# The MLP's first stage by seven products on two levels, with its outer sums kept in SBUF

## Chip, cores and metric

One core of one Trainium2 chip runs the kernel. The metric is the device time of one execution in microseconds (us). The engines are called as in the profile: PE (TensorE, matmuls; PEld its weight loads), ACT (ScalarE), DVE (VectorE), POOL (GpSimd) and SP (SyncE, which only issues DMAs here). Each engine has one queue of instructions.

## The reference

A decoder block on x of 2048 tokens x 1024 channels, all in float32. Attention and a gated MLP branch are merged, projected and added to x (this makes x1); then comes the part that the change is about:

```
h = _rmsnorm(x, norm_pre_mlp[layer])
a = jax.nn.relu(jnp.einsum('bsd,df->bsf', h, w_mlp_in[layer]))
y = jnp.einsum('bsf,fd->bsd', a * a, w_mlp_out[layer])
x = x + _rmsnorm(y, norm_post_mlp[layer])
```

D_FF is 4096. So the MLP's first stage multiplies 2048 x 1024 by 1024 x 4096, takes relu and square, and the second stage multiplies the result by 4096 x 1024.

## The kernel before

Every float32 product is made of three matmuls: each operand is split into a rounded high part (a copy, on ACT as a rule) and the rest (a subtraction, on DVE or POOL); high x high, high x low and low x high are added up in PSUM. The helper `split` (L70 copy on ACT, L72 on POOL, L78 subtraction on DVE or POOL) does it everywhere, so its lines stand for many tiles. `split_in` (L91) loads and splits.

*Part 2* (merge and output). For four chunks of 512 tokens, in the order 2, 3, 0, 1, `merge` makes the gated sum of the branches in eight steps `dt` of 18 matmuls, and `out_block` makes four blocks of 128 tokens of 48 matmuls each: it loads the rows of x (tile xr, SP, L1233), adds the normed product (DVE L1257), stores x1 (POOL's queue, L1260), norms again, and later (`flush`) transposes the result and stores it as h2 in DRAM. `sums_t` loads quarters of h2, makes four sums on POOL (L1291 to L1294) and stores them (POOL's queue, L1296) for the Strassen operands of the MLP. Outside PE the order of this part is the scheduler's; `behind()` puts what is written under it behind the latest instruction of each queue.

*MLP, first stage.* Seven products in place of eight (Strassen in Winograd's form): the contraction is halved (k 0..3 and 4..7 of 128 channels), tokens are halved within each 1024 (512 each), and features go in pairs of 128 (q, 16 pairs). For each half of the tokens and each q, `product` (L1428) makes seven products of 4 x 3 = 12 matmuls of 128x512. The stationary operands are sums of weight blocks (`add_a`: POOL, L1399 to L1402; splits in `split_a`), the moving ones (B11, B21, T1..T4, B22) sums of h2. Products are added up partly in PSUM and partly by DVE (L1453, L1457); each of the four results gets Relu and Square on ACT (L1437, L1438) and is stored to DRAM as s by a DMA that ACT issues (L1434).

*MLP, second stage.* Seven products again, over s and w_mlp_out: `yproduct` (L1957) makes one product of 2 x 3 = 6 matmuls, then DVE adds it to an accumulator (L1962) before PE may write the same bank again. A step is seven products, 42 matmuls, in the order 1, 2, 6, 7, 5, 4, 3; three steps overlap. `sum_s` prepares the stationary sums of the step three ahead: copy and subtraction of 128x768, four POOL sums of 128x256 (L1757 to L1760), two copies and subtractions of 128x512. `ops_of` splits the moving operands of the next group, `sum_w2` (L1713 to L1717) makes their sums on POOL. From here on all queues follow the order in which the code is written (`as_written`):

```
    def as_written():
        t = mybir.EngineType
        return tc.manual_schedule(engines={t.Activation, t.DVE, t.Pool, t.SP})
```

Of the kernel before, what the change touches and what calls it, by code (L numbers as in the profile page):

```python
# [16 lines left out]
P = 128  # L17
S = 2048
D = 1024
# [22 lines left out]
def block_kernel(ctx, tc, a, out):  # L42
# [104 lines left out]
    t_d = dtile([2, P, 4, 4, 512], "td")  # L147
# [985 lines left out]
    gtp = stack(e2, "gtp", 2)  # L1133
# [148 lines left out]
    def sums_t(half, k, pl, tag, tag2, bufs2):  # L1282

        w = pl.tile([P, 2, 512], F32, name=f"tq{half}{k}", tag=tag, bufs=1)
        b11, b12 = w[:, 0], w[:, 1]
        b21, b22 = ((wp3 if pl is not ttp else pl).tile([P, 512], F32, name=f"tq{half}{k}{n}", tag=tag2, bufs=bufs2)
                    for n in range(2))
        t0 = half * HALF
        for t, kk, c in ((b11, k, 0), (b12, k, 1), (b22, k + 4, 1), (b21, k + 4, 0)):
            sp.dma_start(t, h2_d[:, kk, t0 + c * 512:t0 + c * 512 + 512])  # L1290
        pool.tensor_sub(b11, b12, b11)  # L1291
        pool.tensor_sub(b12, b22, b12)
        pool.tensor_sub(b22, b22, b11)
        pool.tensor_sub(b21, b21, b22)  # L1294
        for name, t in (("T1", b11), ("T3", b12), ("T2", b22), ("T4", b21)):
            pool.dma_start(t_d[half][:, T_AT.index(name), k], t)  # L1296

    def merge_sums(dt):
        if dt == 3:
            sums_ahead(0)  # L1300

    def merge_sums_last(dt):
        if dt == 3:
            sums_ahead(3)

    def sums_ahead(k):
        with behind():
            sums_t(1, k, ttp, "tq", "tr", 2)

    chunks = (2, 3, 0, 1)  # L1310
    FIRST = ((0, 0), (1, 0), (0, 1), (2, 0), (1, 1))
    e3, er = ExitStack(), ExitStack()
    cnt = [0]

    def psum_any(name):
# [5 lines left out]
    TERMS = {1: ("A11", "B11"), 2: ("A12", "B21"), 3: ("S4", "B22"), 4: ("A22", "T4"),  # L1321
             5: ("S1", "T1"), 6: ("S2", "T2"), 7: ("S3", "T3")}
    NQ, LEAD, TRAIL = NF // 2, 5, 3
    b_, a_, araw, bank, xs_, u_, c1_, n_u, alone_, sums_ = {}, {}, {}, {}, {}, {}, {}, [0], {}, {}

    def load_b(half, name):

        w = r3.tile([P, 2, 4, 512], F32R, name=f"{name}_{half}", tag=name, bufs=1)
        for k in range(0, 4, 2):
            t0, k0 = half * HALF, k + (4 if name == "B21" else 0)  # L1330
            split_in(w[:, :, k:k + 2], h2_d[:, k0:k0 + 2, t0:t0 + 512], None, "act")
# [774 lines left out]
```

## Time and profile before

| | |
|---|---|
| time, median of 3 runs | 2644.91 us (2641.12 to 2645.22) |
| the profiled execution: span | 2646.3 us |
| PE busy | 2614.2 us (99%), 12458 matmuls |
| DVE, POOL, ACT busy | 1659.3, 1195.3, 1092.9 us |
| part 2 | some 1064 to 1398 us from the start |
| MLP, first stage (L1428) | 1398.6 to 2014 us |
| MLP, second stage (L1957, L1939) | 2014 to 2636 us |

A row of groups reads: line, engine, operation, tiles out<-in, partitions x elements, count | busy us in total, mean ns of one | idle time before them and what ended it. A row of a time-ordered list reads: start, duration (us), engine, line, operation, tiles, count, and in brackets the idle time before it with its releaser; several instructions in a row with one name are merged, and their duration is the whole stretch. ACTq, SPq are the sequencers, which issue DMAs. Matmuls overlap, so a single one looks longer (389 ns) than the distance between two.

### The profile page before, as it was taken

The numbers are of one execution on the slowest core, as the hardware profiler recorded it, in microseconds if no ns is written. First come the engines' busy times: TensorE is split into PE (matmuls) and PEld (weight loads), VectorE is DVE, ScalarE is ACT, GpSimd is POOL, SyncE is SP. The second block draws the span as 40 slices with busy tenths as digits, with TensorE's granted clock in tenths as the row PEclk, the third lists the DMA queues.
The fourth block names the chain that finished last, engine by engine and source line by source line (L and its number), as shares of the span: only waits on it lengthen the run. The fifth ranks groups of instructions, "written<-read, shape, count | busy, mean of one in ns | idle before, by whom it ended". The sixth has DMA issues, their size and how long they took to land. (4 is left out here: it accounts for less than half of the span.)

```text
span 2646.3 us, 35496 instructions
## 1 busy us (share of the span) xinstructions
PE 2614.2 (99%) x12458; PEld 2184.1 (83%) x12458; DVE 1659.3 (63%) x2797; ACT 1092.9 (41%) x2286; POOL 1195.3 (45%) x1082
## 2 busy tenths in 40 slices
PE   9999999999999999999999999999999999999998
PEld 8888888788888877888877888888888888888886
DVE  5676665534443456765667664655438888888866
ACT  5213111254455344544446555655545333323334
POOL 0363354364454554211324572233225677666645
PEclk9999999999999999999999999999999999999999
DMA  8779778988898899744556464744443221222235
GB/s 321 286 243 330 258 233 286 299 278 257 290 292 227 231 292 348 261 140 167 213 194 252 155 219 143 230 124 124 123 136 108 88 85 60 88 88 88 88 117 210
DMA packets 389572, 527.25 MB, mean 199 GB/s; under 512 B 57041, under 2 KB 242129, under 8 KB 388370
## 3 DMA queue, kind: packets, MB, share of 16 engines
q1 hardware_dynamic: 300624, 434.98, 49.8%
q0 software_dynamic: 14992, 51.65, 5.1%
q10 hardware_dynamic: 73778, 38.35, 4.8%
q8 instruction: 98, 1.61, 0.2%
q14 instruction: 80, 0.66, 0.1%
HBM read 341.72 MB, written 183.17 MB: 198 GB/s over the span
## 5 line engine op out<-in xcount | busy, mean ns | idle before, releaser
L1957 PE MATMUL ya<-T_spots,s 128*128 128x512 f32 x1176 | 289.3, 389 | 0.7 <-ACT T_spots L70 0.5
L70 ACT ACTIVATE s<-sraw 128x768 fp32r<-128x768 f32 (+1 forms) x184 | 127.2, 696 | 330.4 <-POOL sraw L1758 155.7
L1957 PEld LDWEIGHTS ya<-T_spots,s 128*128 128x128 f32 x1176 | 220.5, 188 | 47.4 <-ACT T_spots L70 0.9
L78 DVE TENSOR_TENSOR s<-sraw,s 128x512 fp32r<-128x512 f32 x172 | 184.2, 1095 | 8.5 <-ACT s L70 5.9
L1428 PE MATMUL aa<-B,A 128*128 128x512 f32 x768 | 182.3, 390 | 1.5 <-ACT xs L1442 0.9
L1399 POOL TENSOR_TENSOR s<-w1r 128x512 f32<-128x512 f32 x32 | 42.4, 1324 | 306.7 <-DVE S L78 260.1
L724 PE MATMUL g<-opA,spots 128*128 128x512 f32 x672 | 170.8, 398 | 2.3 <-DVE cv L756 1.8
L1428 PEld LDWEIGHTS aa<-B,A 128*128 128x128 f32 x768 | 143.8, 188 | 32.1 <-ACT xs L1442 1.3
L724 PE MATMUL g<-opB,spots 128*128 128x512 f32 x648 | 164.0, 397 | 0.0
L1957 PE MATMUL yc<-T_spots,s 128*128 128x512 f32 x624 | 159.6, 389 | 0.0
L95 PE MATMUL x<-hT_a,wq 128*128 128x512 f32 x384 | 149.7, 390 | 0.0
L96 PE MATMUL x<-hT_a,wq 128*128 128x512 f32 x384 | 149.4, 389 | 0.0
L97 PE MATMUL x<-hT_a,wq 128*128 128x512 f32 x384 | 149.4, 389 | 0.0
L724 PEld LDWEIGHTS g<-opA,spots 128*128 128x128 f32 x672 | 120.9, 188 | 24.7 <-issue 2.2
L78 POOL TENSOR_TENSOR spots<-gr,spots 128x512 fp32r<-128x512 f32 x98 | 128.5, 1315 | 23.1 <-DMA gr<-in_w_in_dram 8.8
L1957 PEld LDWEIGHTS yc<-T_spots,s 128*128 128x128 f32 x624 | 117.1, 188 | 24.3
L724 PEld LDWEIGHTS g<-opB,spots 128*128 128x128 f32 x648 | 116.9, 188 | 21.2
L70 ACT ACTIVATE hl<-r 128x512 fp32r<-128x512 f32 x48 | 30.4, 633 | 236.5 <-POOL r L325 89.0
L974 DVE TENSOR_REDUCE o<-po 128x256 f32<-128x512 f32 x48 | 33.2, 691 | 133.1 <-PE po L973 133.1
L72 POOL TENSOR_SCALAR spots<-gr 128x512 fp32r<-128x512 f32 x86 | 55.4, 645 | 133.5 <-PE g L724 92.2
L1757 POOL TENSOR_TENSOR sraw<-sraw 128x256 f32<-128x256 f32 x56 | 41.9, 748 | 161.8 <-DVE s L78 158.8
L78 POOL TENSOR_TENSOR T_spots<-w2r,T_spots 128x512 fp32r<-128x512 f32 x70 | 104.4, 1519 | 7.3 <-ACT T_spots L70 7.3
(430 smaller groups left out, 6965.1 us busy)
## 6 DMA issues: line engine op xcount, KB each, us to landing
w1r<-in_w_mlp_in_dram SPq DMA_DIRECT2D x64, 512.0 KB, 3.7
sraw<-sd SPq DMA_DIRECT2D x128, 256.0 KB, 3.2
qk<-hl SPq DMA_DIRECT2D x24, 1024.0 KB, 5.6
qq<-qk SPq DMA_DIRECT2D x96, 256.0 KB, 5.2
w2r<-in_w_mlp_out_dram SPq DMA_DIRECT2D x16, 1024.0 KB, 7.9
sd<-u ACTq DMA_DIRECT2D x63, 256.0 KB, 3.7
g<-gated SPq DMA_DIRECT2D x56, 256.0 KB, 5.3
gr<-sgd SPq DMA_DIRECT2D x53, 256.0 KB, 4.5
```

The lines of the kernel that those rows point to most:

```text
L70: act.activation(hi, src, AF.Copy)
L72: pool.tensor_scalar(hi, src, 1.0, 1.0, op0=OP.mult, op1=OP.mult)
L78: (pool if lo_eng == "pool" else dve).tensor_sub(lo, src, f32(hi))
L95: pe.matmul(ps, lh, rh, start=start, stop=False)
L96: pe.matmul(ps, lh, rl, start=False, stop=False)
L97: pe.matmul(ps, ll, rh, start=False, stop=stop)
L724: pe.matmul(p, w[:, l, k], h[:, r, k], start=i in (1, 6, 5, 4) and not k and not m, stop=k == 3 and m == 2, skip_group_check=True)
L974: dve.tensor_reduce(ot[:, :, j * 64:(j + 1) * 64], po.rearrange("p (b h e) -> p b e h", b=4, h=2), axis=AX.X, op=OP.add)
L1399: pool.tensor_add(s1, a21, a22)
L1428: pe.matmul(p, w[:, l, k, :], h[:, r, k, :], start=i in (1, 6, 5) and not k and not n, stop=k == 3 and n == 2, skip_group_check=True)
L1757: pool.tensor_add(a22, a21, a22)
L1957: pe.matmul(p, s[:, l], w[r], start=i in (1, 2, 5) and not m and not o, stop=m == 1 and o == 2, skip_group_check=True)
```

## The change

The first stage gets two levels. The outer level halves the contraction (k), the tokens (1024 each) and the features (16 tiles of 128 each) and makes seven outer products, in the order 1, 2, 6, 5, 3, 7, 4. Each outer product has eight inner steps (`hsteps`), one for each pair of feature tiles, and each inner step is again seven products, over two blocks of 128 channels, 512 tokens and 128 features, of 6 matmuls each (`hproduct`). So a step has 42 matmuls, and it is laid out as in the second stage: the same TIMES, three steps overlapping, `sum_ha` for the stationary sums of the step three ahead, `ops_hb` and `sum_w2` for the moving operands of the next outer product, all queues in written order.

The results of the outer products are kept in sixteen SBUF tiles X of 128x1024: outer product 1 writes X, 6 adds to it, 5 makes its own sum in a staging tile, which POOL adds to X and SP stores to DRAM (m5), and 7 adds to X. 2, 3, 7 and 4 finish outputs: in these, each of the four results of a step gets Relu, Square and a store that ACT issues. Before 4, m5 is loaded and POOL subtracts it from X again (`m5_sub`). In 1 and 5, the first product of each place is copied out of PSUM by ACT; all others are added by DVE.

The weight sums of the outer level (S1 to S4) are made in part 2 by sixteen `w_piece` (POOL) and stored to DRAM; two `t_piece` make the inner token sums for the first outer product. `next_piece` is called after the steps dt 4 and 7 of a merge and after each output block of the first three chunks. The outer token sums (tq) are made by POOL during the first outer product (`outer_load`, `outer_sums`, `outer_store`). The second stage's own products are as before; its tiles lie elsewhere.

The core of the diff (of functions that are not shown, `load_ha` loads a step's weights, `load_hb` an outer product's moving operands, `t_piece` is like `w_piece` for h2, and the old first stage is removed):

```diff
-    t_d = dtile([2, P, 4, 4, 512], "td")
+    t_d = dtile([P, 2, 4, 512], "td")
+    tq_d = {n: dtile([P, 4, 1024], f"tq{n}d") for n in ("T1", "T2", "T3", "T4")}
+    ws_d = dtile([NF // 4, P, 4, 2, 512], "wsd")
+    m5_d = dtile([NF // 4, P, 4, 512], "m5d")
     s_d = dtile([NF // 2, 2, P, 4, 4, P], "sd")
...
+    T_AT, WS_AT = ("T1", "T3", "T4", "T2"), ("S2", "S4", "S3", "S1")
...
+    def w_piece(t):
+        w, v = (ttp.tile([P, 2, 512], F32, name=f"{n}w{t}", tag=n, bufs=1) for n in ("tq", "tr"))
+        for z, n in ((v, t + NF // 2), (w, t)):
+            sp.dma_start(z.rearrange("p a c -> p (a c)"), a["w_mlp_in"][n].rearrange("p k c -> p (k c)"))
+        a11, a12, a21, a22 = w[:, 0], w[:, 1], v[:, 0], v[:, 1]
+        q, f = divmod(t, 2)
+        pool.tensor_add(a22, a21, a22)
+        pool.tensor_sub(a21, a11, a21)
+        pool.dma_start(ws_d[q][:, 2:4, f], v)
+        pool.tensor_sub(a11, a22, a11)
+        pool.tensor_sub(a12, a12, a11)
+        pool.dma_start(ws_d[q][:, 0:2, f], w)
+    W_PIECES = [(w_piece, t) for t in range(NF // 2)]
+    pieces = deque(W_PIECES[:13] + [(t_piece, 0), (t_piece, 1)] + W_PIECES[13:])
+    def next_piece():
+        if pieces:
+            f, n = pieces.popleft()
+            with behind():
+                f(n)
+    def merge_pieces(dt):
+        if dt in (4, 7):
+            next_piece()
+    def last_pieces(dt):
+        if dt in (1, 3, 5):
+            next_piece()
 
...
+    NQ, HQ = NF // 2, NF // 4
+    OPS = ("B11", "B21", "T2", "T3", "T1", "T4", "B22")
+    USE = {1: (0, "B11"), 2: (1, "B21"), 6: (2, "T2"), 7: (3, "T3"), 5: (4, "T1"), 4: (5, "T4"), 3: (6, "B22")}
+    S_AT = {1: 0, 2: 1, 4: 2, 6: 3, 5: 4, 7: 5, 3: 6}
...
+    PLACE = {1: (0, 0), 2: (0, 0), 6: (0, 1), 3: (0, 1), 4: (1, 0), 7: (1, 1), 5: (1, 1)}
+    OUTER = ((1, "A11"), (2, "A12"), (6, "S2"), (5, "S1"), (3, "S4"), (7, "S3"), (4, "A22"))
+    OUTER_B = ("B11", "B21", "T2", "T1", "B22", "T3", "T4")
+    hsteps = [(o, q) for o in range(7) for q in range(HQ)]
+    NH = len(hsteps)
...
+    def sum_ha(n):
+        w = ring(n, f"hs_{n}", [P, 2, 7, 256])
+        raw = hraw_.pop(n)
+        hs_[n] = w
+        split(w[:, 0, :3], w[:, 1, :3], raw[:, :3], "act", "dve")
+        yield
+        a11, a12, a22, a21 = (raw[:, k] for k in range(4))
+        pool.tensor_add(a22, a21, a22)
+        pool.tensor_sub(a21, a11, a21)
+        pool.tensor_sub(a11, a22, a11)
+        pool.tensor_sub(a12, a12, a11)
+        yield
+        for to, k in (((4, 6, 1), (2, 4, 1)), ((3, 7, 3), (0, 2, 1))):
+            to, k = slice(*to), slice(*k)
+            split(w[:, 0, to], w[:, 1, to], raw[:, k], "act", "dve")
+            yield
...
+    def ops_hb(o, j, engs=("dve", "pool")):
+        for m, eng in enumerate(engs):
+            op_w2(key(o, m), OPS[j], eng)
+    def sum_w2(q, part, eng=None):
+        r, e = w2r_[q], eng or pool
+        if part == 0:
+            e.tensor_sub(r[:, 4], r[:, 1], r[:, 0])
+            e.tensor_sub(r[:, 1], r[:, 3], r[:, 1])
+        if part in (1, 2):
+            e.tensor_sub(r[:, 0], r[:, 3], r[:, 4])
+        if part in (1, 3):
+            e.tensor_sub(r[:, 2], r[:, 2], r[:, 0])
...
+    outer_t = {}
+    def outer_load(n):
+        k, c = n % 4, n // 4
+        outer_t[n] = [rx.tile([P, 512], F32, name=f"ot{n}{m}", tag="xs" if n % 2 else "c1", bufs=4) for m in range(4)]
+        for t, kk, t0 in zip(outer_t[n], (k, k, k + 4, k + 4), (HALF, 0, 0, HALF)):
+            sp.dma_start(t, h2_d[:, kk, t0 + c * 512:t0 + c * 512 + 512])
+    def outer_sums(n, which):
+        b11, b12, b22, b21 = outer_t[n]
+        if not which:
+            pool.tensor_sub(b11, b12, b11)
+            pool.tensor_sub(b12, b22, b12)
+        else:
+            pool.tensor_sub(b22, b22, b11)
+            pool.tensor_sub(b21, b21, b22)
+    def outer_store(n):
+        k, c = n % 4, n // 4
+        for t, name in zip(outer_t.pop(n), ("T1", "T3", "T2", "T4")):
+            sp.dma_start(tq_d[name][:, k, c * 512:(c + 1) * 512], t)
+    def hproduct(k, n, i):
+        o, q = hsteps[n]
+        m = OUTER[o][0]
+        j, name = USE[i]
+        which = {1: "a", 6: "a", 7: "a", 4: "a", 2: "b", 5: "c", 3: "c"}[i]
+        if i in (1, 2, 5):
+            bank_[n, which] = psum_any(f"h{which}_{n}")
+        p = bank_[n, which]
+        for kk in range(2):
+            w, b = hs_[n], w2_[(o, kk), name]
+            for z, (l, r) in enumerate(((0, 0), (0, 1), (1, 0))):
+                pe.matmul(p, w[:, l, S_AT[i], kk * P:(kk + 1) * P], b[r], start=i in (1, 2, 5) and not kk and not z,
+                          stop=kk == 1 and z == 2, skip_group_check=True)
+        f, c = PLACE[i]
+        first, last_one = i in (1, 6, 7, 4), i in (2, 3, 4, 5)
+        x_ = X[2 * q + f][:, c * 512:(c + 1) * 512]
+        if m in (2, 3, 5):
+            if first:
+                stage_[n, f, c] = rx.tile([P, 512], F32, name=f"e{n}{f}{c}", tag="c1" if (f, c) == (0, 1) else "xs", bufs=4)
+            t = stage_[n, f, c]
+        else:
+            t = x_
+        if m in (1, 5) and first:
+            act.activation(t, p, AF.Copy)
+        elif m in (2, 3) and first:
+            dve.tensor_add(t, x_, p)
+        else:
+            dve.tensor_add(t, t, p)
+        if not last_one or m in (1, 6):
+            return
+        if m == 5:
+            pool.tensor_add(x_, x_, t)
+            later(k + 2, sp.dma_start, m5_d[q][:, 2 * f + c], t)
+            return
+        if m == 7:
+            t = rx.tile([P, 512], F32, name=f"e{n}{f}{c}", tag="xs", bufs=4)
+        act.activation(t, x_ if m == 7 else t, AF.Relu)
+        act.activation(t, t, AF.Square)
+        fq, half = q + (HQ if m in (7, 4) else 0), 1 if m in (2, 4) else 0
+        act.dma_start(s_d[fq, half][:, :, {(0, 0): 0, (1, 0): 1, (1, 1): 2, (0, 1): 3}[f, c]],
+                      t.rearrange("p (i c) -> p i c", i=4))
+    m5_ = {}
+    def m5_load(q):
+        for f in range(2):
+            for c in range(2):
+                t = m5_[q, f, c] = rx.tile([P, 512], F32, name=f"m5_{q}{f}{c}", tag="c1", bufs=4)
+                sp.dma_start(t, m5_d[q][:, 2 * f + c])
+    def m5_sub(q, f):
+        for c in range(2):
+            x_ = X[2 * q + f][:, c * 512:(c + 1) * 512]
+            pool.tensor_sub(x_, x_, m5_.pop((q, f, c)))
+    def hstep(k, n, i):
+        o, q = hsteps[n]
+        hproduct(k, n, i)
+            if q == 1:
+                if o == 6:
+                    for w in range(2):
+                        load_w2(w)
+                else:
+                    load_hb(o + 1)
+            if q == 3:
+                ops_hb(o + 1, 0)
+            if q in (4, 5):
+                for w in range(2):
+                    sum_w2(key(o + 1, w), 0 if q == 4 else 2, dve if not o else None)
+            q5 = n - 5 * HQ - 3
+            if 0 <= q5 < HQ:
+                m5_load(q5)
+                later(k + 4, m5_sub, q5, 0)
+                later(k + 6, m5_sub, q5, 1)
+        if q == HQ - 1 and USE[i][0] < 6:
+            j = USE[i][0] + 1
+            ops_hb(o + 1, j)
+            if j == 1:
+                for w in range(2):
+                    later(k + 2, sum_w2, key(o + 1, w), 3)
...
+        merge_pieces(dt)
...
-            mg = merge(c, yt, {0: flush, 2: flush}, merge_sums if c == 0 else merge_sums_last if c == 1 else None)
+            mg = merge(c, yt, {0: flush, 2: flush}, last_pieces if n == 3 else merge_pieces)
         for i in range(4):
             b = out_block(c, i, mg, flush_older)
             next(b)
             last.append(b)
-            if n == 2 and i % 2:
-                sums_ahead(1 + i // 2)
+            if n < 3:
...
+    e2.close()
+    l3 = stack(e3, "l3", 1)
+    sm = stack(e3, "sm3", 1)
+    in_order = as_written()
+    in_order.__enter__()
...
+    yorder = []
...
+    TIMES = (0, 3, 4, 8, 9, 12, 13)
+    for n in range(NH):
+        ts = FIRST_TIMES[n] if n < 3 else [7 * n + t for t in TIMES]
+        yorder += [(t, 0, n, i) for i, t in zip((1, 2, 6, 7, 5, 4, 3), ts)]
+    t0 = 7 * NH
...
+    for n in range(8):
+        for d, f, args in ((2, outer_load, (n,)), (6, outer_sums, (n, 0)), (8, outer_sums, (n, 1)), (11, outer_store, (n,))):
+            later(6 * n + d, f, *args)
+    gfin = None
+    for k, (_, stage, n, i) in enumerate(yorder):
+        if not stage:
+            hstep(k, n, i)
+        else:
+            if gfin is None:
...
+            m = n + 3 + (NH if stage else 0)
+            if m < NH + len(ysteps):
+                st = sums_of(m)
                 next(st)
                 next(st)
+                ahead(k, m)
                 at(k + 6, st)
                 at(k + 7, st)
...
-    d["w_mlp_in"] = c(n["w_mlp_in"][0].reshape(KT, P, NF, P).transpose(2, 1, 0, 3))
+    w1 = c(n["w_mlp_in"][0].reshape(KT, P, NF, P).transpose(2, 1, 0, 3))
+    w1[1::2] = w1[1::2][:, :, [2, 3, 0, 1, 6, 7, 4, 5]]
+    d["w_mlp_in"] = w1
```

600 lines of the change are left out of this document (160 added, 440 removed).

## The prediction

> **What bounds the kernel now.** I read the page first, then busy time by stage, then time-ordered lists of ACT, DVE and PE. TensorE (PE) sets the time:
>
> ```profile
> span 2646.3 us, 35496 instructions
> PE 2614.2 (99%) x12458; PEld 2184.1 (83%) x12458; DVE 1659.3 (63%) x2797; ACT 1092.9 (41%) x2286; POOL 1195.3 (45%) x1082
> ```
>
> The stage table (window, its length, busy us with counts for PE, PEld, DVE, ACT, POOL; clock, DMA share, GB/s) takes the MLP's first stage, then its second:
>
> ```profile
> 1500.00:2000.00 500.00, 499.14 (x2199) 412.18 (x2199) 269.46 (x325) 264.73 (x431) 182.19 (x140) 1.00 0.49 155
> 2100.00:2500.00 400.00, 400.00 (x1766) 331.04 (x1765) 331.52 (x432) 131.32 (x201) 272.52 (x271) 1.00 0.25 88
> ```
>
> PE never rests in either, and one matmul takes 400.00/1766 = 0.2265 us. Restricted to L1428, the products of the first stage, the table's sum is
>
> ```profile
> sum 1596.00, PE 611.83 PEld 503.76; mean PE 35.99 PEld 29.63
> ```
>
> By the code these are 2 halves x 16 pairs x 7 products x 12 = 2688 matmuls, 611.8 us (0.2276 each). No other engine binds here, so fewer matmuls pay in full as long as the others keep up.
>
> **The matmuls removed.** The new stage has 7 x 8 steps x 7 products x 6 = 2352 matmuls: 336 fewer, at 0.2265, **-76.1 us**. A step of 42 lasts 9.5 us on PE. The second stage before has the same step (42 matmuls, seven DVE additions, three splits of s, all queues in written order) and keeps PE full with DVE at 331.5/400 and ACT at 131.3/400. So DVE alone fits, and the question is what the first stage lays on top.
>
> **What is added on ACT.** Four of the seven outer products (2, 3, 7, 4 of OUTER) finish outputs: in each step four of the seven DVE additions are followed by Relu, Square and a store, all on ACT's queue. The same chain stands in the first stage before:
>
> ```profile
> 1851.61 0.63 ACT L1437 ACTIVATE u<-u 128x512 f32<-128x512 f32 x1
> 1852.28 0.63 ACT L1438 ACTIVATE u<-u 128x512 f32<-128x512 f32 x1
> 1852.94 0.52 ACTq L1434 DMA_DIRECT2D sd<-u  x1
> 1853.61 0.63 ACT L70 ACTIVATE A<-w1r 128x512 fp32r<-128x512 f32 x1 [0.70 <-PE ab L1428]
> ```
>
> From Relu's start to the next ACT work is 2.00 us: the store's issue takes the queue for 0.67. There were 128 chains before too, but over 612 us. Now 128 stand in 32 steps of 9.5 us.
>
> The splits of operands add
>
> ```profile
> 2267.50 0.85 ACT L70 ACTIVATE s<-sraw 128x768 fp32r<-128x768 f32 x1 [3.42 <-PE yc L1957]
> 2268.25 2.18 ACT L70 ACTIVATE T_spots<-w2r 128x512 fp32r<-128x512 f32 x4
> ```
>
> that is 0.75 for the long copy and 0.52 per short one (2.18 = 3 x 0.52 + 0.63). Per step: four chains 8.0, the split of the stationary sums 0.75 + 2 x 0.52 = 1.8, and 14 copies of ops_hb per eight steps 0.9: **10.7 us of ACT against 9.5 of PE**. Even with no waiting those 32 steps lose 1.2 us each, 38 us.
>
> The Trainium skill, "DMA: Bandwidth & Descriptors", section "Anatomy of one DMA — SWDGE (gpsimd) path", puts a sequencer's dispatch at about 50 ns, and its section "Issuing engines are not separate DMA queues" calls the issue usually small relative to the DMA. The trace differs: 0.52 us, 0.67 to the next work. By the page's figure the loop below would shrink by an estimated 4 x 0.6 = 2.5 us and the time by about 80; I go by the row.
>
> **The loop through ACT and DVE.** The queues wait on each other, and both run in written order. The second stage shows DVE's order (its adds are L1962, its splits L78):
>
> ```profile
> 2257.22 0.69 DVE L78 TENSOR_TENSOR s<-sraw,s 128x512 fp32r<-128x512 f32 x1
> 2257.98 0.69 DVE L1962 TENSOR_TENSOR acc<-acc,yc 128x512 f32<-128x512 f32 x1
> 2258.58 1.55 DVE L78 TENSOR_TENSOR s<-sraw,s 128x512 fp32r<-128x512 f32 x2
> 2260.05 1.33 DVE L1962 TENSOR_TENSOR acc_yt<-acc_yt,ya 128x512 f32<-128x512 f32 x2
> 2262.06 0.69 DVE L1962 TENSOR_TENSOR acc_yt<-acc_yt,yc 128x512 f32<-128x512 f32 x1 [0.67 <-PE yc L1957]
> ```
>
> In steady order the products are 1, 7, 5, 2, 6, 4, 3. Chains follow 5, 2, 4 and 3; a short split comes after 4, another short one and the long one after 3. I lay one turn end to end from the start of ACT's long copy:
> - long copy 0.85, DVE's long subtraction 0.95 (1.55 less 0.60), additions of 1, 7 and 5 at 0.60, 0.60, 0.69: 3.7 us. All this time ACT holds the Relu of 5 at the head of its queue;
> - three chains, 6.0: 9.7;
> - short copy 0.63, its DVE subtraction 0.69, the addition of 3, 0.69, with ACT waiting again: 11.7;
> - the chain of 3, 2.0, and the second short copy 0.52: 14.2.
>
> With the handovers between engines I take **14.5 us per turn**, a bound that PE cannot help. Bounds: 13 if handovers and the waiting DVE work shrink; 15.6 if every subtraction runs at the length that it has beside a busy POOL, here a median of 1062 ns (first row) against 684 at least (second row, min/median/max):
>
> ```profile
> L78 DVE TENSOR_TENSOR T_spots<-w2r,T_spots x9: 1056/1062/1193, 2159.3 to 2473.0; 128x512 fp32r<-128x512 f32 x9
> L78 DVE TENSOR_TENSOR s<-sraw,s x126: 684/953/2049, 2104.9 to 2497.3; 128x512 fp32r<-128x512 f32 x84, 128x768 fp32r<-128x768 f32 x42
> ```
>
> The 14 copies of ops_hb stand in the same queue: 7.3 us per outer product. So one of the four takes 8 x 14.5 + 7.3 = 123.3 against 8 x 9.5 = 76.1: +47.2, and four **+189 us** (bounds 4 x 35.2 = 141 at 13 us a turn, 224 at 15.6). Behind the waiting Relu stand ACT's copies for the next operands, behind those DVE's subtractions and additions, and PE waits for the additions to free its banks.
>
> **The other three outer products** have no chains: product 6 is the second stage's step, and in 1 and 5 ACT takes four of the additions. There POOL is the risk:
>
> ```profile
> L1713 POOL TENSOR_TENSOR w2r<-w2r x14: 1289/1297/1740, 1992.7 to 2445.7; 128x512 f32<-128x512 f32 x14
> L1757 POOL TENSOR_TENSOR sraw<-sraw x56: 731/739/1190, 1989.3 to 2526.9; 128x256 f32<-128x256 f32 x56
> L78 POOL TENSOR_TENSOR T_spots<-w2r,T_spots 128x512 fp32r<-128x512 f32 x70 | 104.4, 1519 | 7.3 <-ACT T_spots L70 7.3
> ```
>
> Product 5: 32 additions into X and 8 operand sums at 1.30 make 52.0, 32 sums of stationaries at 0.74 make 23.7, 7 subtractions at 1.52 make 10.6: 86 against 76, +10. Product 1: 32 outer sums and 2 operand sums 44.2, plus 23.7 and 10.6: 79, +3. In the last step of each, 12 of the 14 operand splits come together, six of them on POOL (9.1 us in a 9.5 us step): another 3 to 4 each. I take **+24** (0 if the prefetch of three steps absorbs it, 40 if each backlog counts in full). The sums of the first operands moved off ACT and DVE cost nothing: L1428's PE was already full. The added loads and stores (m5, tq, ws) meet DMA engines at 155 GB/s in this stage (first table), with up to 348 elsewhere, so 0:
>
> ```profile
> GB/s 321 286 243 330 258 233 286 299 278 257 290 292 227 231 292 348 261 140 167 213 194 252 155 219 143 230 124 124 123 136 108 88 85 60 88 88 88 88 117 210
> ```
>
> **Part 2** (merge and output blocks) takes 16 w_piece and 2 t_piece: four POOL sums at 1.30 and two POOL stores at 0.56, 6.3 us each, 18 x 6.3 = 114 us in place of four pieces of that kind, where POOL was busy 11.88 of 100 us (stage table), a store takes 0.56 (its line), and both queues wait for the x1 rows (who waits for whom: total us, times, longest):
>
> ```profile
> 1150.00:1250.00 100.00, 100.00 (x471) 83.43 (x469) 60.24 (x130) 45.26 (x92) 11.88 (x18) 1.00 0.48 161
> ```
> ```profile
> L1296 POOL DMA_DIRECT2D td<-tq x32: 540/557/574, 1261.9 to 1582.6; - x32
> ```
> ```profile
> POOL x1d L1260 <- DVE xr L1257: 168.5, 15, 34.2
> SPq L1233 <- DMA x1d<-xr: 121.6, 12, 16.2
> ```
>
> A piece stands behind the store of x1 on POOL and behind the load of xr on SP, both of which wait for DVE. A late piece holds the next x1 store, hence SP's next xr load and the y and gate loads queued behind it. The idle 168.5 us are the cover; a block lasts 48 matmuls, 11 us, and a piece 6.3. Price 0 to 25, I take **+8**; below zero is excluded, as PE is full there.
>
> **Sum**: 2646.3 - 76.1 + 189 + 24 + 8 = 2791.2 for the profiled execution. Its span lies 1.4 above the median of 2644.91, so the forecast is **2790 us**, 5.5% slower.
>
> **Rivals.**
> *The copies and Relus keep out of each other's way* (other side, faster). If a turn falls below 9.5 us, PE stays the bound: 2644.9 - 76.1 + 24 + 8 = 2601. For it: ACT was only 264.73/500 busy in this stage. Against: the 10.7 us of ACT alone.
> *ACT's rate without the waits*, 10.7 per step: 2601 + 38 = 2639. It needs DVE's subtractions to get behind the additions in the queue; the written order says otherwise.
> *The clock falls as well.* PE now rests about 5 us in each turn, between products 2 and 6. After a wait of 1.90 us (brackets) the trace shows matmuls 0.43 apart instead of 0.23, with a clock of 0.79:
>
> ```profile
> 1021.07 0.50 PE L95 MATMUL z<-w_z,hT_b 128*128 128x512 f32 x1 [1.90 <-DMA hT_b<-hbd]
> 1023.39 0.63 PE L96 MATMUL z<-w_z,hT_b 128*128 128x512 f32 x1
> 1023.81 0.63 PE L97 MATMUL z<-w_z,hT_b 128*128 128x512 f32 x1
> ```
> ```profile
> 1022.00:1030.00 8.00, 7.63 (x27) 6.20 (x28) 0.88 (x2) 0.60 (x1) 1.02 (x4) 0.79 0.87 318
> ```
>
> Slow for a few us per turn, PE still ends within 14.5 (9.5 + 2 to 3). Slow throughout, a step is 42 x 0.425 = 17.9 us, 32 x 3.4 = +109, 2899. The Trainium skill, "TensorE: Matmul & The Clock Gate", Part 1, has the clock halved after an idle window of about 3.4 us and restored after one busy window, which makes it the harmless kind; the 0.79 above agrees with a short spell.
>
> **How the numbers follow.** The loop: 0.80; fast rival 0.09; ACT's rate alone 0.06; slow clock 0.05. The loop's own bounds give 2644.9 - 76 + 141 + 0 + 0 = 2710 to 2645 - 76 + 224 + 40 + 25 = 2858; a handover's error on 32 turns (20 us) widens that to **2690 to 2880**. The three rivals outside hold 0.20. About 0.2% (5.3 us) is what a measurement can tell: the fast rival and half of the ACT rival are faster (0.12), the other half the same (0.03), the rest slower (0.85).
>
> **What would show it.** Right: in products 2, 3, 7 and 4 a step of 14 to 15 us, PE about 65% busy there with ACT next to it above 80%, Relu waiting for DVE after each long copy, DVE's L78 waiting for ACT, PE waiting for DVE's additions (product 6), a clock below 1.00; in product 6 a step of 9.5. Wrong: PE full in those steps, or a first stage under 600 us in place of 532 + 189 + 24 = 745 (670 to 800).

## The result, and the profile after

The changed kernel takes 2872.07 us (median of 4 runs, 2871.14 to 2874.23) where the kernel before takes 2645.06 (2641.12 to 2645.95): 1.0865 times the time, 95% interval 1.085 to 1.0881. The forecast was 2790 with a range of 2690 to 2880, so the sign and the range held, and 82 us were missing.

From the page after, the span, the engines, the granted clock and two groups:

```profile
span 2870.8 us, 35572 instructions
PE 2642.7 (92%) x12122; PEld 2180.9 (76%) x12122; DVE 1760.0 (61%) x2936; ACT 1129.8 (39%) x2340; POOL 1510.9 (53%) x1402
PEclk9999999999999999998998889988888999999999
L1488 PE MATMUL ha<-spot,hs 128*128 128x512 f32 x1344 | 391.9, 447 | 143.7 <-DVE e L1502 51.2
L79 DVE TENSOR_TENSOR hs<-hraw,hs 128x768 fp32r<-128x768 f32 (+1 forms) x168 | 166.8, 1004 | 198.8 <-ACT hs L71 197.2
```

The 336 matmuls are gone (12458 less 12122). PE's share fell from 99 to 92%, and the last fields say what stands in the loop: PE waits most for DVE's additions (L1502, 51.2 of this row's 143.7 us), DVE's subtractions (L79) wait 197 us for ACT's copies (L71). The stage table after shows where (columns as in the prediction): part 2, outer product 2, outer product 6, the second stage.

```profile
1064.00:1399.00 335.00, 287.55 (x1247) 232.79 (x1247) 203.88 (x340) 137.46 (x251) 162.39 (x156) 0.92 0.73 254
1565.00:1670.00 105.00, 86.18 (x317) 67.82 (x316) 52.66 (x78) 53.70 (x86) 41.29 (x46) 0.86 0.40 125
1690.00:1765.00 75.00, 69.42 (x298) 57.00 (x297) 55.92 (x78) 24.77 (x40) 38.53 (x41) 0.95 0.26 85
2260.00:2620.00 360.00, 360.00 (x1590) 298.01 (x1589) 298.85 (x386) 119.06 (x182) 251.46 (x245) 1.00 0.22 78
```

Outer product 2 finishes outputs and does 317 matmuls in 105 us, 13.9 us per 42. Product 6 finishes none and ran at 9.5 a step but for its first two. The second stage is full again. Part 2 does 1247 matmuls in a stretch in which the kernel before did 1527 (its row stands under the eighth experiment). PE waits there for DVE, which norms the blocks and gates the branches (who waits for whom, 1064 to 1465 us: total us, times, longest; the changed kernel, then the kernel before):

```profile
PE pt L1271 <- DVE y L1266: 18.9, 6, 7.1
PE b L96 <- DVE g L1208: 17.8, 6, 4.4
```
```profile
PE b L95 <- DVE g L1204: 1.4, 1, 1.4
PE pt L1267 <- DVE y L1262: 0.2, 1, 0.2
```

Behind that DVE waits 29.3 us for the rows of x (7.4 before), and ACT 63.5 us for the gates (43.8 before): what SP loads comes late.

By first and last matmul, the first stage ran from 1460.5 to 2236.7 us, 776.2 long, where it had run from 1398.6 to 2014, 615.4 long. It starts 61.9 us later, is 160.8 longer, and 1.8 come after it: the 224.5 us by which the spans differ.

Parts of the loop, as ACT has it in the list in order of time (lines left out are marked):

```profile
1624.78 0.63 ACT L1513 ACTIVATE e<-e 128x512 f32<-128x512 f32 x1 [1.76 <-DVE e L1502]
...
1626.10 0.52 ACTq L1516 DMA_DIRECT2D sd<-e  x1
1626.67 0.63 ACT L71 ACTIVATE hs<-hraw 128x512 fp32r<-128x512 f32 x1 [0.60 <-POOL hb L1438]
1628.66 0.63 ACT L1513 ACTIVATE e<-e 128x512 f32<-128x512 f32 x1 [1.36 <-DVE e L1504]
...
1630.55 1.36 ACT L71 ACTIVATE hs<-hraw 128x512 fp32r<-128x512 f32 x2 [0.60 <-ACT e L1514]
1634.93 0.63 ACT L1513 ACTIVATE e<-e 128x512 f32<-128x512 f32 x1 [3.01 <-DVE e L1504]
...
1636.82 0.63 ACT L1513 ACTIVATE e<-e 128x512 f32<-128x512 f32 x1 [0.60 <-DVE e L1502]
...
1638.98 0.63 ACT L1513 ACTIVATE e<-e 128x512 f32<-128x512 f32 x1 [0.88 <-DVE e L1502]
```

and DVE, which answers it, with one line of PE:

```profile
1627.33 0.69 DVE L79 TENSOR_TENSOR hs<-hraw,hs 128x512 fp32r<-128x512 f32 x1 [2.59 <-ACT hs L71]
1627.94 0.68 DVE L1504 TENSOR_TENSOR e<-e,hc 128x512 f32<-128x512 f32 x1
1631.21 1.69 DVE L79 TENSOR_TENSOR hs<-hraw,hs 128x512 fp32r<-128x512 f32 x2 [2.59 <-ACT hs L71]
...
1638.26 0.69 DVE L1502 TENSOR_TENSOR e<-X,ha 128x512 f32<-128x512 f32 x1 [1.75 <-PE ha L1488]
```
```profile
1633.65 4.58 PE L1488 MATMUL ha<-spot,hs 128*128 128x512 f32 x12 [2.58 <-DVE e L1502]
```

Follow one hand-over: ACT's short copy at 1626.67 releases DVE's subtraction at 1627.33, behind it stands the addition at 1627.94, and that releases the Relu at 1628.66. ACT had waited 1.36 us for it, and DVE 2.59 us for the copy. Each engine holds what the other wants, twice a turn.

Laid end to end on ACT, a turn without any wait for PE is 13.9 us: three times 1.89 for a chain (Relu at 1634.93, the next at 1636.82), 1.99 from the short copy to the Relu that it releases, 1.89 for that chain, 4.38 from the two copies at 1630.55 to the next Relu. On top comes what PE adds. After its rest of 2.58 us it does twelve matmuls in 4.58 us, DVE's addition at 1638.26 waits 1.75 for them, and the Relu at 1638.98 stands 0.88 and not 0.60 after the work before it: 0.28 us. In the turn before, the Relu at 1624.78 stands 1.76 after it, which is 1.16 more.

### The profile page after: what moved, and what is told of

It is laid out like the page before. It is cut to its first block, busy times and chain, and to the rows that moved or that the text cites. A ratio compares the mean times of both kernels' runs of the same rounds, so it can differ in the third digit from the quotient of the medians.

```text
span 2870.8 us, 35572 instructions
## 1 busy us (share of the span) xinstructions
PE 2642.7 (92%) x12122; PEld 2180.9 (76%) x12122; DVE 1760.0 (61%) x2936; ACT 1129.8 (39%) x2340; POOL 1510.9 (53%) x1402
## 5 line engine op out<-in xcount | busy, mean ns | idle before, releaser
L1488 PE MATMUL ha<-spot,hs 128*128 128x512 f32 x1344 | 391.9, 447 | 143.7 <-DVE e L1502 51.2
L1488 PEld LDWEIGHTS ha<-spot,hs 128*128 128x128 f32 x1344 | 291.4, 220 | 227.7 <-issue 89.9
L1806 PE MATMUL ya<-spot,s 128*128 128x512 f32 x1344 | 327.0, 392 | 11.6 <-DVE X_yt L1814 11.6
L1806 PEld LDWEIGHTS ya<-spot,s 128*128 128x128 f32 x1344 | 254.5, 190 | 65.6 <-ACT spot L71 6.6
L79 DVE TENSOR_TENSOR hs<-hraw,hs 128x768 fp32r<-128x768 f32 (+1 forms) x168 | 166.8, 1004 | 198.8 <-ACT hs L71 197.2
L71 ACT ACTIVATE s<-sraw 128x768 fp32r<-128x768 f32 (+1 forms) x184 | 127.2, 696 | 330.7 <-POOL sraw L1676 153.3
L79 DVE TENSOR_TENSOR s<-sraw,s 128x768 fp32r<-128x768 f32 (+1 forms) x176 | 188.2, 1094 | 14.8 <-ACT s L71 13.4
L1488 PE MATMUL hc<-spot,hs 128*128 128x512 f32 x672 | 177.0, 399 | 2.0 <-DVE e L1504 1.0
L1806 PE MATMUL yc<-spot,s 128*128 128x512 f32 x672 | 170.5, 389 | 0.0
L71 ACT ACTIVATE hs<-hraw 128x768 fp32r<-128x768 f32 (+1 forms) x168 | 112.9, 698 | 121.5 <-POOL hraw L1383 36.9
L1488 PEld LDWEIGHTS hc<-spot,hs 128*128 128x128 f32 x672 | 131.5, 196 | 32.9 <-DVE e L1504 1.4
L79 POOL TENSOR_TENSOR spots<-gr,spots 128x512 fp32r<-128x512 f32 x98 | 128.6, 1316 | 23.5 <-DMA gr<-in_w_in_dram 9.2
L79 POOL TENSOR_TENSOR spot<-w2r,spot 128x512 fp32r<-128x512 f32 x86 | 126.8, 1504 | 12.7 <-ACT spot L71 12.7
```

Of the source, the lines that this page charges most:

```text
L71: act.activation(hi, src, AF.Copy)
L79: (pool if lo_eng == "pool" else dve).tensor_sub(lo, src, f32(hi))
L1488: pe.matmul(p, w[:, l, S_AT[i], kk * P:(kk + 1) * P], b[r], start=i in (1, 2, 5) and not kk and not z, stop=kk == 1 and z == 2, skip_group ...
L1806: pe.matmul(p, s[:, l], w[r], start=i in (1, 2, 5) and not m and not o, stop=m == 1 and o == 2, skip_group_check=True)
```

## The experiments

"Step" is the distance between the starts of product 2 in successive steps. PE can run ahead of the loop and then wait for it, so single steps scatter. Of the 32 steps of outer products 2, 3, 7 and 4 in the changed kernel, eleven take 13.8 to 14.2 us; these are called plain. The first two after each change of outer product take 28.8 to 36.5 together, the other thirteen 14.9 to 17.0. Kernels with one run have one time; the others have a ratio to the kernel before, with its interval.

**1. Stores off ACT.**

```diff
-        act.dma_start(s_d[fq, half][...], t.rearrange(...))
+        later(k + 2, sp.dma_start, s_d[fq, half][...], t.rearrange(...))
```

> The stores of the first stage's results are issued by SP two products later, not by ACT. Loop through ACT and DVE (my theory): each turn of the loop holds four store issues of 0.57 us, so a step in outer products 2, 3, 7, 4 falls from 14.2 to about 11.9 us, and the time by some 32 x 2.3 = 74 us to about 2800 us. Rival, ACT's rate alone binds: ACT's work per step falls from 10.2 to 7.9 us, below PE's 9.5, so the step falls to 9.5 and the time to about 2720. Rival, PE at a lowered clock binds (17.9 us per step if the clock stayed halved): ACT does not matter, step 14.2, time 2872.

2804.59 us, stage 712.9, plain steps 11.2 to 11.3. The loop turns without the four issues, 2.9 us sooner: more than 4 x 0.57, the time from an issue to ACT's next work (1626.10 to 1626.67 above). From Relu to Relu it is now 1.20 us for 1.89, 0.69 less. The loop stays: ACT still waits 3.01 and 1.36 us for DVE in a plain turn, so ACT's rate alone is not the answer. The Trainium skill, "DMA: Bandwidth & Descriptors", section "Anatomy of one DMA — SWDGE (gpsimd) path", puts a dispatch at about 50 ns, for DMAs that POOL issues. Here each store that ACT issued cost ACT 0.7 us, and a store of x1 that POOL issues takes POOL's queue 0.57 us.

**2. Low parts behind the copies.** DVE's subtractions and POOL's sums are written one or two products after the copy that they need. ACT's two short copies move as well: they stand together, one product before the place of the first:

```diff
-        split(w[:, 0, :3], w[:, 1, :3], raw[:, :3], "act", "dve")
+        act.activation(w[:, 0, :3], raw[:, :3], AF.Copy)
         yield
+        dve.tensor_sub(w[:, 1, :3], raw[:, :3], f32(w[:, 0, :3]))
...
+            later(k + 1, (dve if eng == "dve" else pool).tensor_sub, w[1], src, f32(w[0]))
```

> DVE's subtractions of a split are written one to two products behind ACT's copies (and the four POOL sums with them), so no addition of DVE stands behind a subtraction whose copy waits in ACT's queue; all work and all stores stay. Loop: with the loop cut, ACT's own work binds, 10.2 to 10.7 us per step in place of 14.2, so the time falls by about 32 x 3.7 = 118 us to some 2750. Rival, ACT's rate alone: the waits never mattered, step stays 14.2, time 2872. Rival, lowered PE clock: the rest of PE per step stays as long, 14.2, time 2872.

2794.33 us, 44 over the 2750 expected; stage 695.6, plain steps 10.7 to 11.3, somewhat over the expected 10.2 to 10.7. With nearly the same instructions as the changed kernel and another order, 3 us of a step are gone. In a plain turn of 11.3 us (1612.30 to 1623.63) ACT now waits once, 1.62 us for DVE after the long copy; the other 9.7 are its own work and issues.

**3. Both.**

> Both edits at once: stores from SP and subtractions behind. Loop: ACT has 7.9 us per step and no ring of waits, so PE binds at 9.5 us per step in all seven outer products; the first stage falls from 776 to some 565 us (532 of matmuls, the rest POOL in products 1 and 5), the time to about 2660. What is left over the kernel before is part 2 (+62 us). Rivals: a lowered clock or DVE's own work (8.5 to 9 us per step) keep the step above 10.5, time above 2700.

2747.24 us, ratio 1.0389 (1.0371 to 1.0406), stage 652.1; 2660 and 565 had been expected. The stage table, in the plain steps of outer product 2 of this kernel:

```profile
1585.00:1640.00 55.00, 54.57 (x238) 44.26 (x238) 41.04 (x58) 39.42 (x66) 29.40 (x32) 1.00 0.56 167
```

PE is full again (54.57 of 55.00) and a plain step takes 9.5 us. So order and store issues together make the plain steps of the loop; outer products 2, 3, 7 and 4 fall from 494.0 to 373.7 us, of which 304.4 are PE's. Of the 69 us left, some 50 lie in the first three and the last step of each, next to the changes of outer product; the rest lies further in, most of it in a step of 16.6 us in product 7 and one of 15.2 in product 4. At the first change, in the list in order of time (PE, then DVE, then the stage table):

```profile
1563.98 5.24 PE L1496 MATMUL ha<-spot,hs 128*128 128x512 f32 x12 [6.55 <-DVE e L1510]
```
```profile
1563.14 0.69 DVE L1510 TENSOR_TENSOR e<-X_yt,ha 128x512 f32<-128x512 f32 x1 [4.34 <-POOL ot L1476]
```
```profile
1555.00:1575.00 20.00, 13.45 (x50) 10.57 (x48) 13.33 (x14) 7.76 (x14) 19.61 (x15) 0.83 0.27 94
```

DVE's addition waits for a staging tile that POOL's outer sums (ot) still hold, and POOL is busy 19.61 of 20 us with those sums and half of the operand splits.

**4. PE kept warm.** Before product 2, in the same four outer products, twenty more matmuls into its bank, written over by the product:

```diff
+        if i == 2 and m in (2, 3, 7, 4):
+            for z in range(20):
+                pe.matmul(p, hs_[n][:, 0, S_AT[i], :P], w2_[(o, 0), name][0], start=True, ...)
```

> Twenty extra matmuls per step in outer products 2, 3, 7, 4, written into product 2's bank just before product 2 itself overwrites it, fill the 4.5 us in which PE rests between products 2 and 6; the result is unchanged. Loop through ACT and DVE: the granted clock there goes from 0.85 to 1.0, but the step stays at 13.5 to 14.2 us and the time within 2850 to 2875, because PE was not what bound. Rival, the lowered clock is part of the bound (products 6 and 4 run at half speed after the rest, and the chain of 4 waits for them): step 12 to 13, time 2800 to 2835. Rival, PE's work binds: 20 x 0.2265 = 4.5 us more per step, time above 2950.

2876.32 us, plain steps 14.1. Its stage table in outer product 2:

```profile
1565.00:1670.00 105.00, 102.56 (x442) 84.72 (x443) 53.98 (x77) 49.72 (x79) 40.66 (x45) 0.96 0.40 126
```

The clock rises from 0.86 to 0.96, PE does 125 matmuls more in the same 105 us, and the plain turn is as long as before. So PE had room for 20 matmuls in a turn, and its own work does not set the loop. What the clock costs this run can't show: 62 matmuls at 0.2265 are 14.04 us, PE is as good as full, and no turn could have fallen below that. It also has no room for the twenty in the short steps behind a change (9.5 and 10.9 us became 14.1), which can hide a gain elsewhere (15.3 to 16.3 became 14.1 in products 2 and 3). The rows above are the better answer: 13.9 us of the turn wait for no matmul, and the slow ones add 0.28 us to one turn and 1.16 to another.

**5. Pieces copied.** Part 2's w_piece becomes two copies from DRAM to DRAM out of POOL's queue, without tiles, SP loads or sums (the summed weight operands are then plain weights).

```diff
+        pool.dma_start(ws_d[q][:, 2:4, f], a["w_mlp_in"][t + NF // 2]...)
+        pool.dma_start(ws_d[q][:, 0:2, f], a["w_mlp_in"][t]...)
```

> Leaves out the weight sums of the outer level: the sixteen w_piece copy the weights from DRAM to DRAM by POOL's queue, with no SBUF tiles, no SP loads and no POOL sums (so the S operands are not sums); the two t_piece stay. Theory for part 2: its 62 us more come from SP's queue, which stands at the load of a piece until the piece before it is summed and stored out of the one buffer (106 us of such waits), with loads of y, gates and xr behind. Then part 2 falls from 396 to 335 to 350 us and the time from 2872 to 2810 to 2825. Rival, DMA traffic: the bytes moved stay nearly the same, so part 2 stays above 380 us.

2843.42 us, between what the two theories gave; the first stage starts at 1428.4: half of the 61.9 us is gone, half stays. The DMA view of 1064 to 1400 us (tiles, queue, count, KB each, median us from issue to landing), before, here, and in the changed kernel:

```profile
xr<-in_x_dram SPq DMA_DIRECT2D x16, 512.0 KB, 4.0
h2d<-tt POOLq DMA_DIRECT2D x28, 256.0 KB, 3.6
```
```profile
xr<-in_x_dram SPq DMA_DIRECT2D x13, 512.0 KB, 7.0
h2d<-tt POOLq DMA_DIRECT2D x24, 256.0 KB, 6.7
```
```profile
xr<-in_x_dram SPq DMA_DIRECT2D x13, 512.0 KB, 4.6
h2d<-tt POOLq DMA_DIRECT2D x24, 256.0 KB, 4.5
```

The rows of x take 3.0 us longer to land beside the copies. That fits the half that stays here, but no run took the traffic alone away, so it is argued and not shown. In the changed kernel they take only 0.6 us longer than before, so the half that stays here need not be a part of its loss.

**6. Piece loads on POOL's queue.**

```diff
-            sp.dma_start(z..., a["w_mlp_in"][n]...)
+            pool.dma_start(z..., a["w_mlp_in"][n]...)
```

> The loads of the pieces of part 2 are issued by POOL in place of SP; sums, stores and bytes are as in the changed kernel. If SP's queue was what held PE, part 2 falls to 340 to 360 us and the time to 2820 to 2840; POOL then waits for its own loads (about 5 us a piece), which its idle time of some 200 us covers. Rival, POOL's own work (18 x 6.3 us of sums in front of the x1 stores) holds the xr loads: part 2 stays above 380 us, or grows.

2877.1 us, first stage from 1461.7: no gain. SP no longer waits for piece stores, but its wait for the x1 store before the next rows of x grew from 67.3 us (x11) to 181.2 (x15). The kernel before has 121.6 us (x12) of this wait with PE full, so its size alone does not measure a loss. The theory that the loads' waits in SP's queue are the loss falls; that the hold moved with the loads fits, but is not shown.

**7. Experiments 1, 2 and 6 together.**

> Stores from SP, subtractions behind, and the pieces' loads from POOL's queue. The three add up if they are separate costs: the run with the first two took 2747 us with part 2 at 396 us; with part 2 at 350 the time is 2700. Still slower than before by 55 us: POOL at the changes of outer product (the steps there take 14 to 21 us in place of 9.5) and what is left in part 2. Rival, they overlap: above 2730.

2745.9 us, ratio 1.0389 (1.0372 to 1.0407), stage 652.1, from 1459.5: the third experiment again. The sixth adds nothing here either.

**8. No weight pieces.**

```diff
-    pieces = deque(W_PIECES[:13] + [(t_piece, 0), (t_piece, 1)] + W_PIECES[13:])
+    pieces = deque([None] * 13 + [(t_piece, 0), (t_piece, 1)])
...
-            src = ws_d[q][:, WS_AT.index(name)]
+            src = a["w_mlp_in"][2 * q:2 * q + 2, :, 0:4].rearrange(...)
```

> All sixteen w_piece are left out of part 2; outer products with a summed weight operand read plain rows of w_mlp_in in place of the sums, so this kernel leaves the weight sums out. The two t_piece stay. Two theories of the 62 us that part 2 lost (397.5 against 334.0 us from 1064): (a) the pieces themselves, by what they put ahead of x's rows and the gates, in whichever queue: then part 2 is back at 334 to 342 us, the first stage starts near 1400 and the time is 2872 - 57 = 2815 (2805 to 2820). (b) something else that the change did to part 2 (its tiles lie elsewhere and the order of the gates' loads differs): then it stays at 365 us or more even without pieces, as it did with the copied pieces, and the time is 2840 or more. The first stage itself should not move: 776 us.

2809.38 us, first stage from 1397.0 and 776.2 long. The stage table of part 2, before and then without pieces:

```profile
1064.00:1399.00 335.00, 329.98 (x1527) 274.08 (x1526) 219.07 (x416) 154.27 (x295) 70.62 (x87) 0.99 0.57 197
```
```profile
1064.00:1399.00 335.00, 329.31 (x1524) 274.03 (x1523) 213.25 (x421) 156.44 (x301) 60.23 (x73) 0.99 0.53 182
```

1524 matmuls against 1527: the whole loss of part 2 is the sixteen pieces, and the first stage is the same without it.

**9. No POOL splits at the ends of outer products 1 and 5** (on top of the third):

```diff
-            ops_hb(o + 1, j, k)
+            ops_hb(o + 1, j, k, ("dve", "dve" if o in (0, 3) else "pool"))
```

> The kernel with both edits (stores issued by SP two products later, low parts written behind) has plain steps of 9.5 us and loses its time at the changes of outer product, where POOL was busy for the whole of the change 1 to 2. Here the fourteen operand splits at the ends of outer products 1 and 5 take all their subtractions on DVE, none on POOL (seven of 1.52 us each leave POOL, seven of 0.7 come to DVE). If POOL binds at these two changes: the steps there fall from 18.6 to about 12 and from 17.9 + 11.1 + 15.0 to about 31 in sum, the stage from 652 to 635 us, the time from 2747 to about 2730. If DVE binds there (it makes the additions that free PE's banks): steps the same or longer, 2745 to 2765. If the changes wait on something else, the staging tiles or the loads of the next operands: no change, 2743 to 2750.

2741.92 us, ratio 1.0375 (1.0358 to 1.0393), stage 647.9. At the change 5 to 3 POOL was it: three steps of 17.9 + 11.1 + 15.0 became 11.6 + 11.9 + 10.1, though the step before them grew from 11.5 to 15.4. At 1 to 2 the step fell only from 18.6 to 16.6. The table there shows why:

```profile
1555.00:1575.00 20.00, 15.55 (x59) 12.36 (x58) 19.39 (x23) 8.54 (x16) 12.34 (x11) 0.83 0.41 142
```

POOL fell from 19.61 to 12.34 us, and DVE is now busy 19.39 of 20. At this change the work fills whichever of the two engines gets it. The runs of the two kernels overlap (2740.74 to 2745.9 and 2742.37 to 2749.41 us), so the gain of 5 us in the time is not clear of their spread.

**10. Half pieces, loaded one place ahead.**

```diff
+        w, v = (ttp.tile([P, 2, 256], F32, ..., bufs=2) for n in ("tq", "tr"))
         sp.dma_start(z, ...)
+        yield        # sums and stores follow at the next place
```

> Every piece is cut in two halves of 256 columns, each with two buffers of half the size, and its loads are issued one place ahead of its sums and stores (a place: after nearly every step of a merge and after every output block); the sums and the bytes moved are as in the changed kernel. POOL's work per whole piece grows from 6.3 to about 8.2 us. Theory (a), order: the 62.9 us of part 2 are waits inside a piece. POOL waits for the piece's load, SP waits for the store of the piece before, and what stands behind both (the store of x1, the next load of x's rows, the gates) is held. With loads one place ahead neither wait is left: part 2 takes 335 to 350 us, the first stage starts near 1405, the time is 2872 - 55 = 2817 (2808 to 2825). Theory (b), load: POOL's added work or the added traffic is what holds the x1 stores, whatever the order: part 2 stays at 385 us or more, and the time at 2860 or more. Copied pieces without sums gave half (365), so a value between 355 and 380 would say that both take part.

2887.45 us, part 2 409.7: worse. The waits of SP's queue in part 2:

```profile
SPq L1309 <- DMA wsd<-trw: 77.4, 25, 6.7
SPq L1309 <- DMA wsd<-tqw: 41.5, 21, 5.4
```

SP still waits 46 times for piece stores, of which there are now twice as many: the second buffer was not free in time either. The test did not take away the wait that it was meant to, so it decides nothing about the order; as a remedy it fails.

**11. 1, 2, 9 and 10 together.**

> All that helped together: stores issued by SP two products later, low parts written behind, no POOL splits at the ends of outer products 1 and 5, half pieces loaded one place ahead. The parts lie one after the other in time, so the gains should add: 2742 less what the half pieces alone bring to part 2. By the order theory that is 2742 - 55 = 2687 (2680 to 2700), still 1.6% over the kernel before, since the changes of outer product cost more than the removed matmuls bring; by the load theory about 2740.

2753.88 us, ratio 1.0421 (1.0402 to 1.044): 12 us over the ninth, and neither of the two expected times (2687 and 2740): the half pieces cost about what they cost alone (15 us there).

**12. POOL left to the pieces.** The changed kernel's trace shows the round that a piece makes. POOL, then SP's loads:

```profile
1171.30 1.29 POOL L1309 TENSOR_TENSOR trw<-tqw,trw 128x512 f32<-128x512 f32 x1 [3.50 <-DMA tqw<-in_w_mlp_in_dram]
...
1177.95 0.73 POOL L1313 DMA_DIRECT2D wsd<-tqw  x1 [0.42 <-POOL tqw L1312]
1178.67 0.57 POOL L1264 DMA_DIRECT2D x1d<-xr  x1
```
```profile
1167.16 0.33 SPq L1305 DMA_DIRECT2D tqw<-in_w_mlp_in_dram  x1
1168.40 0.33 SPq L1237 DMA_DIRECT2D xr<-in_x_dram  x1
...
1182.12 0.33 SPq L1305 DMA_DIRECT2D tqw<-in_w_mlp_in_dram  x1
```

Load at 1167.16, first use 4.1 us later, last store at 1177.95, next load 4.2 us after that: 15.0 us for this piece with one buffer, where PE needs 48 x 0.2265 = 10.9 for an output block. The loads of tqw follow each other at 14.0 to 23.6 us in all of part 2, but for one gap of 44.1 in which the t_piece lie. And x1's store stands behind the piece (1178.67), the next rows of x behind that store. On top of the ninth, POOL issues the pieces' loads as well, and ACT the stores of x1 and h2:

```diff
-        pool.dma_start(x1_d[t0:t0 + P, :], xt)
+        act.dma_start(x1_d[t0:t0 + P, :], xt)
...
-            pool.dma_start(h2_d[:, k:k + 4, t0:t0 + P], tt[:, k:k + 4])
+            act.dma_start(h2_d[:, k:k + 4, t0:t0 + P], tt[:, k:k + 4])
```

> On top of the kernel with DVE at the changes (2741.92 us), POOL is left alone with the pieces of part 2: it issues their loads, sums and stores, and the stores of x1 and h2 that stood in its queue are issued by ACT (16 of x1, 32 of h2, about 0.6 to 0.8 us each: 34 us of ACT, which is 41% busy there). The half pieces had fallen as a test: SP still waited for stores 46 times, and the doubled store issues filled POOL. What the changed kernel's trace shows instead is a round: a piece's load takes 4.1 us to land, its sums and stores 6.7, and the next load waits 4.2 us more for the store to land, 15.0 us per piece against 11.1 us per output block, in the queues that also hold x's rows, x1 and h2. Theory (round): if nothing but pieces stands in the held queue, the rounds hold nobody: 18 x 15 = 270 us fit into part 2, it takes 335 to 350 us, and the time is 2742 - 55 = 2687 (2680 to 2700). Rival (load): POOL's sums beside DVE or the added traffic slow everything, or ACT's added issues do: part 2 stays at 370 us or more, the time at 2715 or more.

2724.67 us, ratio 1.0306 (1.0289 to 1.0324): the fastest of the twelve, but part 2 takes 382.0 us, as the rival said, and not 335 to 350. The parts of part 2 tell more. Over PE's 0.2265 per matmul, the output blocks of the chunks and the merges lose (merge, blocks, merge, blocks and so on) 13.9, 9.3, 3.8, 3.1, 15.9, 3.7, 4.7 and 24.4 us, against 14.0, 10.3, 16.8, 15.4, 10.5, 16.2, 11.0 and 2.0 in the ninth. The kernel before loses about 13 in the first merge and 1.8 to 3.9 in each other place. So in four of the middle places the hold is mostly gone, and a new one stands at the end. Moving the loads alone had brought nothing (6), so the stores of x1 and h2, which no longer stand behind the pieces, are the likelier part; no run moves them alone. SP's queue, ACT and PE at the end:

```profile
SPq L1373 <- DMA wsd<-trw: 20.8, 1, 20.8
```
```profile
1407.07 0.84 ACT L1379 ACTIVATE hs<-hraw 128x768 fp32r<-128x768 f32 x1 [18.63 <-DMA hraw<-in_w_mlp_in_dram]
```
```profile
1416.72 0.79 PE L96 MATMUL o<-wo,mg 128*128 128x512 f32 x1 [14.42 <-DVE y L1257]
```

The first stage's first weights wait 20.8 us for the last piece's store. Left alone, the pieces follow every 14 to 25 us and end late. The copy of those weights already stands in ACT's queue, ahead of the last output blocks' work: ACT waits 18.63 us for it, DVE for ACT, and PE, still in an output block, 14.42 us for DVE. What one merge still loses (15.9) was not followed up.

## Why the prediction was right, and where its sizes failed

**Matmuls removed, -76.1.** Right: 336 are gone, and PE works at 0.2265 wherever it is fed.

**The loop, +189.** Right in mechanism, and in sum. The four outer products took 122.9 + 118.4 + 126.6 + 126.1 = 494.0 us against 493.2 forecast. That they agree to 0.8 us is in part luck: at a plain turn of 14.1 for 14.5, what eight such turns leave of the mean of 123.5 is 10.7 us a product, where 7.3 were allowed. Experiments 1 to 3 show that the written order and the store issues both make the turn: with either one mended it is about 11 us, with both PE's 9.5.

**The rivals.** The fast one is refuted by the changed kernel. ACT's rate alone fails too: the turn of 13.9 us holds 9.6 of ACT's work and issues besides its waits of 1.36 and 3.01, and with the order mended (2) there is still one wait for DVE in the 11 us. The clock fell to 0.86 as the third rival said. It was taken for harmless within a turn, and is nearly so: it adds 0.28 and 1.16 us to the two turns shown. Two signs were read wrongly. PE was to be about 65% busy, and the table shows 86.18 of 105, 82%: a matmul took 0.272 us there and not 0.2265. ACT was to be over 80% busy, and the table shows 53.70 of 105. The busy column leaves out the issue of stores and all waiting; the 10.7 us of ACT's work in a turn of 14.5 would never have been over 74%.

**The other three outer products, +24.** Too small. The stage loses 776.2 - 2352 x 0.2265 = 243.5 us over PE's work; less 189.6 in the loop, 53.9 are here: 26.0 in products 6 and 5 (93.0 + 85.2 less 2 x 76.1), 27.9 in product 1 with the start and the end of the stage. The prediction charged product 5 with 10, product 1 with 3, and each of the three with 3 to 4 for the splits of its last step. Product 5 lost 9.1, less than charged. The step that failed is the one that took product 6 for the second stage's step: it lost 16.9 in its first two steps, 18.6 and 17.4 us long, where PE waits 12.0 us for DVE's additions. With the order mended and the stores off ACT (3), product 6 takes 82.2 us, so some 11 of the 16.9 have the same two causes as the loop. Of product 1, steps 2 to 4 took 13.9, 17.0 and 14.3 us. The ninth experiment puts part of the changes on POOL; the rest is not settled.

**Part 2, +8.** The term that failed most: 61.9 us, all of it the pieces (8). The prediction saw the two queues and what stands in them, and then took POOL's idle 168.5 us as cover and 6.3 us as the price of a piece. That is POOL's time. The round of the piece shown is 15.0 us, with two DMA landings and one buffer, and in that time the loads and stores of part 2 stand behind it. That the round is the cause is argued: the twelfth experiment cleared four of the middle places, but the sixth and the tenth brought nothing, and no version of the pieces gave part 2 back. What share the added traffic has stays open.

**The range.** That it held is luck in part. Both small terms fell outside their own bounds (53.9 for 0 to 40, 61.9 for 0 to 25). With those bounds the prediction's sum ended at 2858; the 20 us added for a handover, and a loop 34 us under its upper bound, covered the rest.

In sum 2646.3 - 76.1 + 189.6 + 53.9 + 61.9 + 1.8 (after the stage) - 6.6 (what the stage before took beyond its matmuls) = 2870.8, the span after.

## What to carry to other kernels

Where two engines run in written order and hand work to each other, lay one turn end to end: its length is a bound of its own, whatever the busy shares say, and moving an instruction one or two places down its queue can take much of it away. Price work that is slipped in beside a stage by the time that it stands in a queue, its DMA landings and its single buffer counted, and not by the busy time of the engine that does it; here the busy time gave 8 us and the pieces cost 61.9. Cost the changes between phases by themselves: here, once the plain turns were mended, most of what stayed in the four outer products lay there, and no version that was tried reached the kernel before. And when spare work is added to an engine to see whether it binds, add up what it then has to do: here it filled the turn to 14.04 us and could show no shorter one.

## What the runs showed of the hardware

A store's issue held ACT for 0.57 us to its next work, and taking four of them off ACT shortened a turn by 2.9 us. After a rest of 6.55 us, twelve matmuls took 5.24 us where 12 x 0.2265 are 2.7, at a granted clock of 0.83 around it (third experiment). The Trainium skill, "TensorE: Matmul & The Clock Gate", Part 1, says that the clock halves after an idle window of about 3.4 us. The trace agrees in the halving, but shows slow matmuls after a shorter rest as well: twelve in 4.58 us after 2.58 us of rest in the changed kernel. Twenty spare matmuls a turn brought the clock from 0.86 to 0.96 without moving the time (2876.32 us in one run, 2872.07 without them).
